# In-projection of a hybrid encoder layer: the first two Strassen products of all sixteen feature pairs ahead of the rest, from un-normalised input

## The chip, the cores and the metric

The kernel runs on one core of a Trainium2 chip. The metric is the time of one launch on the device in microseconds. Of the kernel before there are three timed runs, with a median of 1248.74 us (1247.93 to 1249.16), and one profiled execution.

## The reference

One layer over 1024 tokens of width 1024, all in float32. What matters here is its beginning:

```python
h    = rms_norm(x, norm_mix_pre)          # x * rsqrt(mean(x^2)) * gain
proj = h @ w_in                           # 1024 x 1024 by 1024 x 4096
q, k, v, u, gates = split(proj, [512, 1024, 1536, 2048])
y_a  = chunk_band_attention(q, k, v, rel_bias) @ w_attn_out
y_b  = multiscale_pool(u, w_pool_group, pool_scale) @ w_pool_out
g_a, g_b = split(sigmoid(gates + b_gate), 2)
x = x + rms_norm((g_a * y_a + g_b * y_b) @ w_o, norm_mix_post)
x = x + rms_norm(conv_gated_ffn(rms_norm(x, norm_ffn_pre)), norm_ffn_post)
```

The scale of a row, rsqrt(mean(x^2)), is one number per token. A product with the un-normalised input times the gain can therefore be multiplied by the token's scale afterwards.

## The kernel before

Features lie on partitions and tokens along the free axis. w_in has 32 blocks of 128 features; they are worked on in 16 pairs (`IN_PAIRS`): pairs 0 to 3 and 8 to 11 are blocks of the gates, 4 and 5 of u, 6 and 7 of v, 12 to 15 one block of q with one of k. The input is cut into quadrants B11, B12, B21, B22 (first index: half of the 1024 input features; second: half of the tokens), and the weights of a pair into w11, w12, w21, w22. Float32 precision comes from splitting each operand into a high and a low part (`split`, `split_w`: the cast to the high part on ScalarE, the low part by a subtraction on VectorE). One product of a 128x512 weight block with a 512x512 operand is then 12 matmuls (`mm3`): four blocks of the inner dimension, each high by high, high by low, low by high.

A pair would need eight such products; the class `Pair` makes seven, after Strassen and Winograd: p1 = w11·B11, p2 = w12·B21, p5 = s1·T1, p6 = s2·T2, p3 = s4·B22, p7 = s3·T3, p4 = w22·T4. Here s1 to s4 are sums of the weight blocks (`first`, `sums`, on GpSimd, for the first pairs on VectorE) and T1 to T4 differences of quadrants. Products accumulate in a bank of PSUM where their sum is wanted: p1, p6, p7 and p4 in bank X, p5 and p3 in bank Y, p2 in bank Z. p1 is copied out of X (c1), p1 + p6 as u2, p5 as c5; the four results are evicted as p1 + p2, Y + u2, X + c5 and X. `run_pair` sets the order p1, p2, p6, p3, p7, then p5 of the next pair, then p4.

Pairs 0 and 1 are not made that way. They are done first, by eight products per pair (192 matmuls, line 414, tiles `i`), from un-normalised input for all four quadrants (XR), since the scales of the rows (`scales`, `spread`, tiles R0 and R1 for the two halves of the tokens) are not there yet; the eviction multiplies by R. Then the input is normalised, the operands B11, B21 and T1 to T4 are made, and pairs 2 to 15 run. Pairs 4 and 5 are begun early: their p1 and p2 run in bank m while VectorE makes T1 and T2, their c1 is kept in SBUF, and p6 later starts a new sum, to which VectorE adds c1 at the evictions (line 248 and others).

The gates go through a sigmoid and into DRAM (sig_d, stores from ScalarE's queue), q and k are split and stored, v is transposed, u is stored and read again for the pooled path, whose products (mxp) stand between pairs 8 to 12. The weights of a pair (`win`, 1 MB) are loaded from SP's queue, which works in order, into a ring of six buffers that later also holds the pooled results. The order of each engine comes out of a planner that goes by priorities and expected durations; `high_priority` pulls a block forward. After the in-projection come attention, the output products and the FFN, whose up-projection uses the same class `Pair`, with three pairs begun early.

## Time and profile before

| | us |
|---|---|
| median of three runs | 1248.74 |
| the profiled execution | 1248.39 |
| its span, first to last instruction | 1246.6 |
| TensorE (PE) busy | 1231.2 |
| VectorE (DVE) busy | 939.8 |
| ScalarE (ACT) busy | 657.3 |
| GpSimd (POOL) busy | 282.9 |
| first matmul | 6.71 |
| attention's first scores (pst) | 332.02 |

The granted clock of TensorE is 0.999 over the span. Busy time of TensorE is from the start of a matmul to its end with overlaps counted once, so the share of 99% says that it hardly ever waited, not that it could go no faster. L414 is line 414 of the kernel before; the lines 78, 79 and 86 are in the helpers `split` and `mm3` and belong to every product, so that the tile's name tells which one: `X_i` is bank X of the in-projection, `X_u` that of the up-projection. In names, wh and wl are the high and low parts of weights, xq a quadrant of the input, `first` and `wfirst` the weights of the first products.

### The profile page before, as it was taken

To read this page: it belongs to the slowest core of one execution; us is meant where nothing else is said; L and a number is where in the kernel's file an instruction comes from. 1 tells how busy PE (TensorE), PEld (TensorE's weight loads), DVE (VectorE), ACT (ScalarE), POOL (GpSimd) and SP (SyncE) were. 2 spreads that over 40 slices of the span, in tenths; PEclk is the share of its full clock that TensorE was granted. 3 is DMA by queue.
4 is the path that set the end of the run, shared out by engine and by line. 5 is a ranking of instruction groups with operands and counts; after the bars stand their busy time and mean duration, and the time that the engine had idled before them with its cause. 6 is when DMAs were issued, how large, how long until landed. Compare 5 with 4: busy or idle time off the path is not lost.

```text
span 1246.6 us, 16208 instructions
## 1 busy us (share of the span) xinstructions
PE 1231.2 (99%) x5756; PEld 1023.7 (82%) x5756; DVE 939.8 (75%) x1503; ACT 657.3 (53%) x1149; POOL 282.9 (23%) x229
## 2 busy tenths in 40 slices
PE   7999999999999999999999999999999999999997
PEld 6888888888889888888788888888888888888886
DVE  5996346876588887756799988666676676899968
ACT  6663345564487774434545555455545555445553
POOL 0004222232255546000003443334334300000000
PEclk9999999999999999999999999999999999999999
DMA  9336024335988746412344333122231216903103
GB/s 355 138 131 231 26 89 184 129 131 188 297 277 269 263 154 242 152 73 86 112 148 153 130 110 126 61 102 73 79 101 56 88 68 221 377 18 101 35 1 136
DMA packets 57329, 178.11 MB, mean 143 GB/s; under 512 B 5344, under 2 KB 5984, under 8 KB 52384
## 3 DMA queue, kind: packets, MB, share of 16 engines
q1 hardware_dynamic: 51264, 164.23, 37.3%
q10 hardware_dynamic: 4752, 8.39, 1.8%
q0 software_dynamic: 1232, 4.46, 0.9%
q8 instruction: 45, 0.74, 0.2%
q14 instruction: 36, 0.29, 0.1%
HBM read 128.30 MB, written 48.76 MB: 142 GB/s over the span
## 4 chain that ended last, share of the span: by engine, by line
PE 89%; DVE 8%; issue 1%; ACT 1%; DMA 0%; DVEq 0%; SPq 0%; ACTq 0%
PE X_u L86 16%; PE X_i L86 12%; PE Y_u L86 9%; PE X L86 7%; PE wops L1063 7%; PE Y_i L86 6%; PE i L414 4%; PE Z_u L86 4%; PE y L86 4%; PE ybp L86 4%; PE Y L86 3%; PE Z_i L86 3%; PE f L863 3%; PE tp L838 2%; PE m_u L86 2%; PE pst L795 2%
## 5 line engine op out<-in xcount | busy, mean ns | idle before, releaser
L1187 DVE SCALAR_TENSOR_TENSOR hc<-hu,cv,hc 128x1022 f32<-128x1022 f32 (+1 forms) x88 | 122.7, 1396 | 27.0 <-ACT hc L1182 26.8
L78 ACT CAST wh_u<-s_u 128x512 fp32r<-128x512 f32 x88 | 54.4, 619 | 92.4 <-PE X_u L86 41.7
L79 DVE TENSOR_TENSOR wl_u<-s_u,wh_u 128x512 fp32r<-128x512 f32 x88 | 66.5, 757 | 30.0 <-ACT wh_u L78 30.0
L79 DVE TENSOR_TENSOR wl_i<-s_i,wh_i 128x512 fp32r<-128x512 f32 x56 | 42.7, 763 | 37.3 <-ACT wh_i L78 37.1
L78 ACT CAST wh_i<-s_i 128x512 fp32r<-128x512 f32 x56 | 34.6, 622 | 59.9 <-PE X_i L86 21.9
L78 ACT CAST wh_u<-wup 128x512 fp32r<-128x512 f32 x60 | 37.3, 622 | 52.3 <-PE Y_u L86 27.3
L1182 ACT ACTIVATE hc<-hu,cv 128x1024 f32<-128x1024 f32 x44 | 54.6, 1244 | 12.2 <-DVE hu L1131 11.4
L208 POOL TENSOR_TENSOR s_u<-s_u,wup 128x512 f32<-128x512 f32 x19 | 26.6, 1403 | 131.1 <-DVE wl_u L79 131.1
L204 POOL TENSOR_TENSOR s_u<-wup 128x512 f32<-128x512 f32 x19 | 33.7, 1775 | 74.7 <-DVE wl_u L79 74.7
L204 POOL TENSOR_TENSOR s_i<-win 128x512 f32<-128x512 f32 x11 | 15.9, 1446 | 150.8 <-DVE wl_i L79 112.8
L817 POOL TENSOR_SCALAR pe<-pe,st 128x640 f32<-128x640 f32 (+4 forms) x58 | 40.3, 699 | 42.2 <-DVE st L815 28.3
L813 ACT ACTIVATE pe<-sm,st 128x640 f32<-128x640 f32 (+2 forms) x64 | 44.3, 694 | 8.1 <-DVE st L811 7.8
L79 DVE TENSOR_TENSOR ptl<-tp,pth 128x512 fp32r<-128x512 f32 (+3 forms) x80 | 43.0, 552 | 7.4 <-ACT pth L78 6.6
L210 POOL TENSOR_TENSOR s_u<-wup 128x512 f32<-128x512 f32 x19 | 40.7, 2141 | 27.2 <-DVE wl_u L79 27.2
L1192 ACT ACTIVATE hc<-hc 128x1024 f32<-128x1024 f32 x22 | 23.4, 1062 | 39.8 <-DVE hc L1187 39.8
L78 ACT CAST pth<-tp 128x512 fp32r<-128x512 f32 (+3 forms) x80 | 36.4, 474 | 14.8 <-PE tp L838 10.5
L86 PE MATMUL ybp<-mx,wh_yb 128*128 128x512 f32 x128 | 43.4, 414 | 0.0
L78 ACT CAST wh_i<-win 128x512 fp32r<-128x512 f32 x38 | 23.4, 622 | 37.4 <-PE X_i L86 22.8
L79 DVE TENSOR_TENSOR wl_u<-wup,wh_u 128x512 fp32r<-128x512 f32 x60 | 42.1, 702 | 0.7
L811 DVE CUSTOM_DVE_ANT_0 sm<-pst,bt 128x640 f32<-128x640 f32 (+2 forms) x64 | 40.5, 651 | 2.7 <-issue 1.5
L863 PE MATMUL f<-ptl,vv 128*128 128x256 f32 x144 | 36.5, 287 | 0.0
L838 PE MATMUL tp<-ident,pe 128*128 128x128 f32 x240 | 36.2, 275 | 0.1
(503 smaller groups left out, 4169.9 us busy)
## 6 DMA issues: line engine op xcount, KB each, us to landing
wup<-in_w_up SPq DMA_DIRECT2D x22, 1024.0 KB, 5.0
win<-in_w_in SPq DMA_DIRECT2D x14, 1024.0 KB, 5.8
g_d<-hc SPq DMA_DIRECT2D x20, 512.0 KB, 2.7
sig_d<-d ACTq DMA_DIRECT2D x32, 256.0 KB, 2.0
a<-g_d SPq DMA_DIRECT2D x8, 1024.0 KB, 10.9
b<-in_w_dn SPq DMA_DIRECT2D x8, 1024.0 KB, 12.3
x<-in_xn SPq DMA_DIRECT2D x8, 512.0 KB, 11.5
v_d<-vt SPq DMA_DIRECT2D x8, 512.0 KB, 3.1
```

The costliest lines, as they stand in the source:

```text
L78: r = A.copy(hi, src)
L79: (eng or V).tensor_tensor(lo, src, hi.bitcast(F32), ALU.subtract)
L86: nc.tensor.matmul(ps, a[i], b[i], start=start and i == 0 and p == 0, stop=stop and i == n - 1 and p == 2, skip_group_check=True,)
L204: self.eng.tensor_tensor(self.s1, self.w21, self.w22, ALU.add)
L210: self.eng.tensor_tensor(self.s3, self.w11, self.w21, ALU.subtract)
L414: nc.tensor.matmul(acc[b, t], w[:, b], x[:, k], start=i == k == p == 0, stop=i == 1 and k == 3 and p == 2, skip_group_check=True)
L813: A.activation(pe[:, :n], sm[:, :n], AF.Exp, scale=-1.0, bias=st[:, 0:1], accum_out=st[:, 1:2])
L838: nc.tensor.transpose(tp[:, c * P:(c + 1) * P], pe[:, b * P:(b + 1) * P], ident)
L863: nc.tensor.matmul(fo, vv[:, kb, e].rearrange("p a d -> p (a d)"), t[:, s], start=s == slots[0] and x == 0, stop=s == slots[-1] and x == 1)
L1063: nc.tensor.matmul(ps[:, 512 * c:512 * c + 512], a[k // 4][:, k % 4, sl], wo[k][b][:, 512 * c:512 * c + 512], start=k == 0 and x == 0, sto ...
L1182: A.activation(c, hu, AF.Identity, scale=cv[:, C_CW + 88 + b:C_CW + 89 + b], bias=cv[:, C_CB + b:C_CB + b + 1])
L1187: V.scalar_tensor_tensor(c[:, n:], hu[:, :S - n], cv[:, w:w + 1], c[:, n:], ALU.mult, ALU.add)
```

## The change

The two pairs of plain products are gone; all sixteen pairs are made of seven products. But p1 and p2 of all pairs are run first, in a stage of their own:

- The first 96 matmuls are p1 and p2 of pairs 0 to 3, from the un-normalised input of the first half of the tokens (XR, only B11 and B21). p1 goes to banks X and Y, p2 to Z and m; ScalarE copies p1 out (c1), VectorE adds both.
- For pairs 4 to 15, p1 and one product later p2 accumulate in one bank (X, Y and Z in turn), with p1 copied out between them. The eviction multiplies the sum by R0. Half of a pair's weights (`w12`, 512 KB) is loaded for this.
- c1 of each pair is stored to DRAM (c1_d, ScalarE's queue), un-normalised.
- R0, R1, the normalised quadrants and the operands T1 to T4 and B22 are made during this stage.
- Then each pair runs its other five products, p6, p3, p7, p5 of the next pair, p4. c1 is loaded back (SP's queue, one buffer), and VectorE writes c1·R0 into bank X before p6, which accumulates onto it. So u2 and c5 become plain copies on ScalarE, as for a pair that is not early.
- XR lies where attention's first two heads have their operands later; these are loaded from q_d and k_d (`load_head`) after pair 14 in program order.
- The FFN's three early pairs get c1 into the bank in the same way, by a copy on ScalarE without a scale (`seed`).
- The pooled path stands two pairs apart, at pairs 6, 8, 10 and 12.

In the whole program TensorE has 5732 matmuls in place of 5756.

```diff
@@ class Pair
+        def begin(self, w, c1):
             self.early, self.c1 = True, c1
+            if w is None:
+                return
         def p1(self):
             if self.early:
-                self.X = self.bank("m")
+                self.X = self.bank(self.tags[0])
...
         def p2(self):
+            if self.tags != "mm":
+                self.prod(self.X, self.w12, "B21", False, "2")
+                self.evict(0, 0, self.X, None)
+                return
...
         def p6(self):
             if self.early:
                 self.X = self.bank("X")
-            self.prod(self.X, self.s2, "T2", self.early, "6")
-            if self.early:
+            if self.scale is not None:
+                V.tensor_tensor(self.X, self.c1, self.scale, ALU.mult)
+            elif self.seed:
+                A.copy(self.X, self.c1)
+            self.prod(self.X, self.s2, "T2", self.early and not self.seed, "6")
+            if self.early and not self.seed:
                 V.tensor_tensor(self.u2, self.X, self.c1, ALU.add)
             else:
                 A.copy(self.u2, self.X)
...
@@ the in-projection
-        XR = {(0, 0): two("T1", "XR00")}
+        XR = [(hd.tile([P, 4, 512], F32R, tag=f"qk{i}", name=f"XRh{i}"),
+               Halves(*[hd.tile([P, 2, 512], F32R, tag=f"{x}{i}", name=f"XRl{i}{x}") for x in ("kl", "bt")]))
+              for i in range(2)]
...
+        def load_w12(n):
+            w12[n] = tmp.tile([P, 1024], F32, tag="o", bufs=4, name=f"w12_{n}")
+            nc.sync.dma_start(w12[n], w_in[n][:, :1024])
...
+        def keep_p1(n):
+            A.dma_start(c1_d[n], pairs[n].c1)
+
+        def turn(n):
+            p = pairs[n]
+            p.weights(raws[n])
+            p.c1 = tmp.tile([P, 512], F32, tag="c1", name=f"c1b_{n}", bufs=1)
+            nc.sync.dma_start(p.c1, c1_d[n])
+            p.scale = Rb[0]
+            p.evict = evict_in(IN_PAIRS[n])
+            return p
+
+        acc = [[psp.tile([P, 512], F32, tag=tag, name=f"first{i}{b}") for b, tag in enumerate(t)]
+               for i, t in enumerate(("XXYY", "ZZmm"))]
+            for i in range(2):
+                for k in range(4):
+                    split_raw(i, k)
+                    products(acc[i], i, k)
+            for n in range(4):
+                A.copy(begin(n).c1, acc[0][n])
...
+            scales(0)
+        sums = [wr[0][:, n] for n in range(4)]
+        for n in range(4):
+            V.tensor_tensor(sums[n], acc[1][n], pairs[n].c1, ALU.add)
...
+        for n in range(5, NP):
+            if n + 3 < NP:
+                load_w12(n + 3)
...
+            p.p1()
+            keep_p1(n)
+            with tc.high_priority():
+                p.prep("2", p.w12)
+            pairs[n - 1].p2()
+            for x in extra.get(n, ()):
+                x()
...
+        for pi in range(2, NP):
+            for n in (pi + 1, pi + 2):
+                if n < NP and n not in raws and (pi < 9 or n == pi + 1):
+                    load_win(n)
+            if pi in (7, 11):
+                    mx[x].append(rawp.tile([P, 2, S], F32R, tag="raw", name=f"mx{x}{pi}"))
+            after = turn(pi + 1) if pi + 1 < NP else None
+            run_pair(pair, after,
+                     {"p6": lambda: split_yb(0), "p7": lambda: split_yb(1)} if after is None else (), True)
...
+            if pi == 14:
+                load_head(0)
+                load_head(1)
@@ the FFN's early pairs
-            p.evict, p.first_product, p.early_prep = evict, first, prep
+            p.evict, p.first_product, p.early_prep, p.seed = evict, first, prep, True
```

The queue of SP around the last pairs' weights. Before (win13 to win15 are the weights of pairs 13 to 15, wg the pooled path's weights, u its input, q_d and k_d stores of results):

```order
L521 DMA u3_2043<-u_d_69 128x1024
L545 DMA wg2_2189<-in_w_pg 128x128
L337 DMA win13_2230<-in_w_in 128x2048
L472 DMA q_d_66<-hl_2270 128x2x512
L545 DMA wg3_2386<-in_w_pg 128x128
L337 DMA win14_2408<-in_w_in 128x2048
```

The same stretch with the change (c1b_13 and c1b_14 are the c1 of pairs 13 and 14 on their way back, qk0 the first head's q):

```order
L553 DMA u3_2453<-u_d_69 128x1024
L577 DMA wg2_2429<-in_w_pg 128x128
L622 DMA c1b_13_2455<-c1_d_74 128x512
L622 DMA c1b_14_2592<-c1_d_74 128x512
L378 DMA win13_2451<-in_w_in 128x2048
L503 DMA q_d_66<-hl_2497 128x2x512
L378 DMA win14_2590<-in_w_in 128x2048
L503 DMA k_d_67<-hl_2520 128x2x512
L359 DMA qk0_2846<-q_d_66 128x1024
```

The loads of c1 for two pairs now stand ahead of the weights of pair 13, and the first load for a head among the stores.

VectorE at the same place with the change (X_i13 is the bank of pair 13 into which c1·R0 is written; wl_5_i13 the low part of the weights s1 of its p5; d31_1 and d0_1, d4_1 evictions of pairs 11 and 12):

```order
L530 TENSOR_TENSOR d31_1_2381<-X_i11_2326,p5_i11_2264 128x512
L80 TENSOR_TENSOR wl_3_i12_2480<-s4_i12_2386,wh_3_i12_2479 128x512
L80 TENSOR_TENSOR wl_7_i12_2502<-s3_i12_2387,wh_7_i12_2501 128x512
L256 TENSOR_TENSOR X_i13_2597<-c1b_13_2455,R0_361 128x512
L80 TENSOR_TENSOR mx111_2320<-mo2_2439,mx011_2319 128x512
L530 TENSOR_TENSOR d0_1_2495<-Y_i12_2391,u2_i12_2459 128x512
L502 SCALAR_TENSOR_TENSOR hl_2497<-d0_1_2495,hl_2497 128x512
L80 TENSOR_TENSOR wl_5_i13_2533<-s1_i13_2457,wh_5_i13_2532 128x512
L530 TENSOR_TENSOR d4_1_2517<-X_i12_2460,p5_i12_2392 128x512
```

The write into the bank stands among the splits and evictions of the pair before; in the order of the kernel before there is no such row, and in its place stand the splits of p1 and p2 of each pair (wl_1, wl_2).

385 lines of the change are left out of this document (167 added, 218 removed).

## The prediction

> **What bounds the kernel now.** I read first the page's busy times, then the list of waits for TensorE (engine, line, releaser: total us, times, longest), then the chain of waits over the in-projection.
>
> ```profile
> PE 1231.2 (99%) x5756; PEld 1023.7 (82%) x5756; DVE 939.8 (75%) x1503; ACT 657.3 (53%) x1149; POOL 282.9 (23%) x229
> PE i L414 <- ACT w0s L78: 6.7, 1, 6.7
> PE X_u L86 <- ACT wh_u L78: 0.5, 1, 0.5
> PE X_i L86 <- ACT u_i L250: 0.4, 1, 0.4
> ```
>
> TensorE is busy for 1231.2 of 1246.6 us, and of the 15.4 us it is not, 6.7 us are the start. No later wait is longer than 0.5 us. Every matmul taken away therefore shortens the run by its pace, as long as no new wait takes its place. The pace stands in the chain (start, duration, what) and in TensorE's timeline:
>
> ```profile
> 6.71 22.21 PE i L414 x84
> 109.15 2.72 PE Y_i L86 x12
> 31.96 0.63 PE L414 MATMUL i<-XR01h,w0s 128*128 128x512 f32 x2
> 44.19 0.60 PE L433 MATMUL rps<-ident,bc 128*128 128x128 f32 x4
> 44.55 0.71 PE L414 MATMUL i<-XR01h,w0s 128*128 128x512 f32 x2
> 54.56 0.39 PE L86 MATMUL X_i<-B11h,wh_i 128*128 128x512 f32 x1
> ```
>
> A product of 12 matmuls takes 2.72 us, so one matmul 0.2267 us. The 0.39 us of the single matmul in the last row is its latency, not its pace; I do not use it. The second half of the plain products (96 matmuls, token half 1) runs from 31.96 to 54.56: 22.60 us, of which 0.36 (44.19 to 44.55) are the four small transposes, against 96 x 0.2267 = 21.76. So this loop loses 0.48 us.
>
> Then I asked how near the other engines are to being late, by windows (window, length, then busy us with counts of PE, PEld, DVE, ACT, POOL, then clock, share of DMA, GB/s):
>
> ```profile
> 30.00:100.00 70.00, 70.00 (x311) 57.70 (x310) 67.77 (x96) 47.72 (x71) 0.01 (x1) 1.00 0.44 161
> 90.00:170.00 80.00, 80.00 (x355) 66.30 (x354) 40.62 (x58) 28.19 (x46) 22.89 (x17) 1.00 0.31 112
> 250.00:332.00 82.00, 81.96 (x361) 67.45 (x360) 53.09 (x71) 42.67 (x73) 21.80 (x16) 1.00 0.56 188
> 332.00:350.00 18.00, 18.00 (x112) 15.80 (x111) 16.20 (x49) 12.45 (x32) 6.96 (x16) 1.00 0.89 291
> 680.00:700.00 20.00, 19.11 (x84) 15.20 (x83) 19.89 (x22) 9.91 (x14) 7.38 (x4) 1.00 0.51 171
> ```
>
> From 30 to 100 us VectorE is busy 67.77 of 70 us and TensorE still never waits. From 90 us on VectorE is half idle, and the DMA engines are half idle until attention starts at 332.
>
> **The change, part by part.**
>
> *Fewer matmuls.* Before: two pairs by plain products (192 matmuls) and 14 pairs of seven products (14 x 84 = 1176), together 1368. After: 16 pairs of seven products, 16 x 84 = 1344; the first 96 of these are p1 and p2 of pairs 0 to 3. That is 24 fewer: -24 x 0.2267 = **-5.44 us**.
>
> *The slow loop.* The 22.60 us loop is gone and its work done in products at the pace of 2.72 us: **-0.48 us**. The other half, 6.71 to 31.96, stays as it is in order and operands (weights and input arrive in the same order, except one 512 KB load ahead of the row-wise input, which only the row scales need).
>
> *The row scales.* R0 and R1 are now computed while p1 and p2 of pairs 4 to 7 run. Their transposes on TensorE take 0.36 us each before and after. The new thing is what R0 stands behind: on ScalarE its root comes after the copy of p1 of pair 4.
>
> ```profile
> L219 ACT COPY p_i<-Y_i 128x512 f32<-128x512 f32 x12 | 7.0, 580 | 0.4 <-ACT d L503 0.4
> 22.30 0.30 ACT L302 ACTIVATE rs_s<-ssq,eps 128x4 f32<-128x4 f32 x1
> 23.64 0.43 DVE L430 COPY bc<-rst 128x512 f32<-128x512 f32 x1
> ```
>
> The first 96 matmuls end near 31.6 (31.96 less the transposes, which move), p1 of pair 4 near 34.4. Copy 0.58, root 0.30, from the root's end (22.60) to the copy bc (23.64) 1.04, and 0.43 for it: 36.8 us. TensorE comes to the transposes, which stand behind 10 matmuls of p1 of pair 5, at 31.6 + 2.72 + 2.27 = 36.6. Bounds for such a wait: 0, if matmul and copy overlap, and 1 us, if the squares of the rows are late by that; 0.3 for R0, by the sum and a little for the signals between the engines, and the same for R1, which is placed likewise: **+0.6 us**.
>
> *VectorE in the stage of first products.* It adds p1 and p2 of pairs 0 to 3, multiplies 16 first blocks by R0, splits 24 weight blocks, normalises the input and makes the T operands. From row 20 of its order up to the split of the weights that p6 of pair 1 needs, I count 101 instructions: 7 subtractions and 8 splits of 128x1024 (T1, T2, B22, T3) at 1.22 us, 16 normalisations at 0.745, 56 others of 128x512 at 0.68 to 0.76 (38.8 us in all), 12 tiny steps of the row scales and two copies bc (about 2.4 us together):
>
> ```profile
> L79 DVE TENSOR_TENSOR wl_i<-s_i,wh_i 128x512 fp32r<-128x512 f32 x56 | 42.7, 763 | 37.3 <-ACT wh_i L78 37.1
> L440 DVE SCALAR_TENSOR_TENSOR xq<-xq,gn,R 128x512 f32<-128x512 f32 x16 | 11.4, 745 | 3.0 <-ACT R L435 3.0
> L462 DVE TENSOR_TENSOR xq<-xq,xq 128x1024 f32<-128x1024 f32 x8 | 9.5, 1221 | 0.0
> ```
>
> The sum is 71.4 us. It has from 31.5 to about 109.8 us, 78.3 us. Before, 67.8 of 70 us were carried without a wait; so 71.4 of 78.3 should be: 0. If VectorE does come late, the cover is gone and each us goes to TensorE (rival B).
>
> *p1 into the bank.* Before each p6 VectorE writes c1 x R0 into the bank. No row shows this form; it is a 128x512 write with two inputs, as below, so 0.69 us (between the copy's 0.58 on ScalarE and 1.22 for twice the size). It replaces nothing on TensorE, and in the stretch from 90 us VectorE is half idle:
>
> ```profile
> L248 DVE TENSOR_TENSOR u_i<-X_i,c 128x512 f32<-128x512 f32 x2 | 1.4, 692 | 2.5 <-PE X_i L86 2.5
> ```
>
> There are two X banks. The bank of p6 of pair n is free when p4 of pair n-2 has been evicted, a full pair (five products, 13.6 us) earlier. Cost 0 as long as the c1 load is there: 256 KB land in about 2.0 us (the row sig_d below), one issued per pair.
>
> *The queue of SP, the one place where I expect a new wait.* The loads of c1 stand in SP's order between the 1 MB weight loads, and there is one buffer for them. The load c1b_14 must wait for VectorE's write X_i13 from c1b_13; that must wait until ScalarE has read p4 of pair 11 from the bank. Behind c1b_14 stands win13, whose own buffer is free some 11 us before. Before, no pair's weights stood behind such a load:
>
> ```profile
> 246.62 0.33 SPq L337 DMA_DIRECT2D win<-in_w_in  x1
> 269.93 0.57 SPq L337 DMA_DIRECT2D win<-in_w_in  x1
> 287.16 0.34 SPq L337 DMA_DIRECT2D win<-in_w_in  x1
> 276.10 1.82 POOL L204 TENSOR_TENSOR s_i<-win 128x512 f32<-128x512 f32 x1 [10.39 <-DMA win<-in_w_in]
> 292.36 1.50 POOL L204 TENSOR_TENSOR s_i<-win 128x512 f32<-128x512 f32 x1 [7.91 <-DMA win<-in_w_in]
> L503 ACT ACTIVATE d<-d,cv 128x512 f32<-128x512 f32 x18 | 13.0, 724 | 10.6 <-DVE d L485 10.2 <-DVE s_i L208 0.4
> L78 ACT CAST wh_i<-win 128x512 fp32r<-128x512 f32 x38 | 23.4, 622 | 37.4 <-PE X_i L86 22.8 <-PE Y_i L86 10.1 <-PE i L414 4.2
> win<-in_w_in SPq DMA_DIRECT2D x14, 1024.0 KB, 5.8
> sig_d<-d ACTq DMA_DIRECT2D x32, 256.0 KB, 2.0
> ```
>
> The last two win loads of before took 276.10 - 269.93 = 6.2 and 292.36 - 287.16 = 5.2 us until GpSimd began, and GpSimd already waited for them; p1 and p2 of the same pair (5.44 us) covered that. Now they come first and no longer cover it. Call t the end of p4 of pair 11. Sigmoid 0.72, seed 0.69, two issues 0.33 each: win13 starts near t + 2.0 or 2.1. With 5.2 to 6.2 us to land, 1.5 for s1 on GpSimd, 0.62 for the cast and 0.69 for the low part, of which the first two matmuls cover 0.45, p5 of pair 13 may start at t + 4.4 + landing, t + 9.6 to t + 10.6. It is due at t + 1.36 (six pooled matmuls) + 3 x 2.72 = t + 9.5. So a wait of 0.1 to 1.1 us; I take 0.7, by the median landing of 5.8: **+0.7 us**. Queued behind it on ScalarE are the casts of p4 of pair 12, and on VectorE its evictions; all of them move with TensorE. Bounds: 0 if the load is quick, 6.9 if it takes the 12 us that a load takes under a full DMA (rival A). The weights of pairs 14 and 15 are issued some 5 us before they would be late, so I cost them at 0.
>
> *More traffic.* c1 out and back (16 x 256 KB each way, 8.4 MB), half-weights of ten more pairs (5.2 MB), full weights of pairs 0 and 1 (2.1 MB): 15.7 MB in 325 us, 48 GB/s on top of 110 to 190, at a DMA share of 0.3 to 0.56. Hidden, with the exception above. ScalarE issues 16 stores more (about 0.4 us each, 6.4 us): it is busy 47.7 of 70 us, so that too is hidden.
>
> *Attention's heads.* They are loaded earlier. TensorE was busy 18.00 of 18 us from 332 on, so nothing is gained.
>
> *FFN.* Three early pairs there get c1 copied into the bank by ScalarE and lose VectorE additions. From 680 to 700 VectorE is full (19.89 of 20) and TensorE 0.89 short. Bounds 0 to -0.9; since only nine additions go, I take **-0.3 us**.
>
> Sum: -5.44 - 0.48 + 0.6 + 0.7 - 0.3 = **-4.92 us**. The profiled execution took 1248.39 (span 1246.6 and 1.8 around it); it would take 1243.5, the span 1241.7. The median of the runs, 1248.74, is 0.35 above the profiled one: 1248.74 - 4.92 = **1243.8 us**.
>
> **The rivals.** About 0.2%, 2.5 us, is what a measurement of this kernel can tell from no change.
>
> *A, slower: a late load of win13 stalls TensorE.* Place: p5 of pair 13. The stage from 250 us on has a DMA share of 0.56; at five products per pair in place of seven the same weights and stores come in 5/7 of the time, with c1 loads on top and the heads' loads next to it: share near 0.8. For: with a share of 0.89 after 332 us a 512 KB load took 12.0 us.
>
> ```profile
> sgb<-sig_d SPq DMA_DIRECT2D x2, 512.0 KB, 12.0
> 6.71 2.07 PE L414 MATMUL i<-XR00h,w0s 128*128 128x512 f32 x4 [6.71 <-ACT w0s L78]
> 13.09 1.09 PE L414 MATMUL i<-XR00l,w0s 128*128 128x512 f32 x4
> ```
>
> At 12 us the wait is 4.4 + 12 - 9.5 = 6.9 in place of 0.7: 1243.8 + 6.2 = 1250.0. After a long wait TensorE may start slow, as at the beginning: the 16 matmuls that started from 6.71 to 13.09 took 6.38 us in place of 16 x 0.2267 = 3.63, 2.75 more. I count that in, since nothing shows that it stays away: 1252.8, which is slower. It decides (8.1 us of wait, slow start included) from a landing of 10.5 us. Against: the load's own row has a median of 5.8. The Trainium skill, "TensorE: Matmul & The Clock Gate", section "HAM oscillation — how this bites in real kernels", says that a TensorE idle for more than about 3.4 us falls back to half clock and has to warm up again; by that the wait of 6.9 us gives the 1252.8, and one of 0.7 us costs nothing beside itself. No row after the start shows a gap that long, so the trace agrees only in that the slow matmuls stand right behind the first one.
>
> *B, no change that can be measured: VectorE is late.* Place: between 90 and 115 us, where the split of T3 and T4, the sums of weights for pairs 0 to 2 and the first two seeds meet. On average VectorE stood idle for 37.3 / 56 = 0.67 us before a split of weights, waiting for ScalarE's cast. If 16 of this stage's splits wait like that, 10.7 us, the reserve of 78.3 - 71.4 = 6.9 us is used up and 3.8 go to TensorE: 1247.6. For: VectorE is the fullest engine there, and works in order. Against: instructions that stand back to back come in less than their 0.69 us,
>
> ```profile
> 95.01 0.69 DVE L79 TENSOR_TENSOR wl_i<-s_i,wh_i 128x512 fp32r<-128x512 f32 x1
> 95.61 0.69 DVE L485 TENSOR_TENSOR d<-X_i,p_i 128x512 f32<-128x512 f32 x1
> ```
>
> 0.60 from start to start, and those 0.67 us are from the stage in which VectorE is half idle.
>
> *C, the full gain.* No new wait: -5.44 - 0.48 - 0.9 = -6.8, so 1241.9. For: margins I called close are all positive. Against: win13.
>
> *D, the change doesn't do what it says.* TensorE's order holds 5732 matmuls in place of 5756, so the 24 are gone; that leaves no time for this rival.
>
> **How the numbers follow.** Forecast (waits of 0.5 to 3 us): 0.58, 1242.5 to 1245.9. C: 0.13. B: 0.19, of which 0.05 still end faster than 1246.2. A: 0.10, of which 0.08 end above 1251.2. Faster by over 0.2% (below 1246.2): 0.58 + 0.13 + 0.05 = 0.76; within: 0.14 + 0.02 = 0.16; slower: 0.08. The range: C's end less a little, 1241, up to 1249.5, which takes in B with its uncertainty; it leaves out A and the far end of C.
>
> **What would show it.** The matmul rows of the in-projection sum to 1344 and attention's first scores (pst) start near 327 in place of 332.0. TensorE's list of waits has one entry for Y of p5 with the low or high part of s as releaser, 0 to 1.2 us, and GpSimd's s1 waits for DMA win at pair 13 longer than before. VectorE is near 95% busy from 30 to 100 with no wait of TensorE behind it. The window 680 to 700, moved by the shift, has less than 0.9 us idle. Wrong would be: a wait of TensorE for VectorE between 90 and 115 us of more than 2 us (B), or one of more than 3 us near pair 13 (A), or a pace of products other than 2.72 us.

## The result, and the profile after

The changed kernel takes 1261.06 us (median; 1258.28 to 1264.13), the kernel before beside it 1248.40 (1247.23 to 1249.16). The ratio is 1.0102, with a 95% interval of 1.0087 to 1.0116: slower by 1.0%, 12.7 us, where 4.92 us less were predicted. The profiled execution took 1261.29, its span is 1259.5. One of the four runs of experiment 1 below took 2071.72 us at a mean granted clock of 0.557, and its median is that of the other three.

Busy times of the page after, to be held against 1231.2 us of PE and a span of 1246.6 before:

```profile
PE 1228.8 (98%) x5732; PEld 1018.8 (81%) x5732; DVE 934.6 (74%) x1500; ACT 662.0 (53%) x1167; POOL 300.3 (24%) x236
```

The 24 matmuls are gone and PE is busy for 2.4 us less, but it is now idle for 30.7 us in place of 15.4. The list of waits for TensorE after (releaser: total us, times, longest) says for whom:

```profile
PE first L454 <- ACT w0s L79: 6.9, 1, 6.9
PE Y_i L87 <- ACT wh_i L79: 4.6, 1, 4.6
PE X_i L87 <- DVE d L530: 3.8, 2, 2.7
PE X_i L87 <- ACT u_i L263: 3.3, 2, 2.2
PE X_u L87 <- DVE hu L1150: 1.3, 2, 0.8
PE vps L544 <- DVE vt L80: 1.1, 1, 1.1
PE Y_i L87 <- DVE wl_i L80: 0.8, 1, 0.8
PE mxp L87 <- DVE pdl L80: 0.6, 1, 0.6
PE rps L473 <- DVE bc L470: 0.5, 2, 0.3
```

Before, no wait but the first was over 0.5 us. Now there is one of 4.6 and a row of them from 0.6 to 2.7, for VectorE or for ScalarE. Those of the in-projection lie in two places (hu belongs to the FFN). The windows after (columns as in the prediction):

```profile
100.00:205.00 105.00, 105.00 (x471) 86.80 (x470) 50.73 (x79) 44.25 (x76) 35.02 (x25) 1.00 0.48 168
205.00:320.00 115.00, 105.38 (x463) 84.85 (x462) 85.86 (x112) 58.03 (x99) 46.04 (x27) 1.00 0.50 172
320.00:343.00 23.00, 18.42 (x71) 14.59 (x70) 8.33 (x13) 7.95 (x14) 2.18 (x3) 0.85 0.79 266
```

and the same from the trace before:

```profile
100.00:205.00 105.00, 105.00 (x481) 86.97 (x480) 48.36 (x72) 38.92 (x68) 31.94 (x24) 1.00 0.29 110
205.00:320.00 115.00, 114.54 (x501) 93.59 (x500) 82.69 (x113) 63.94 (x110) 32.65 (x22) 1.00 0.46 161
```

Up to 205 us TensorE is full in both. From 205 to 320, while the pooled path runs, it loses 9.6 us, and here VectorE is busy for 85.9 of 115 us and GpSimd for 46.0 in place of 32.7. In the last 23 us before attention it loses another 4.6, and the clock granted is 0.85.

The ledger goes by TensorE's rows, from start to start, each matmul at its pace of 0.2267 us; "lost" is what lies over that:

| | us |
|---|---|
| fewer matmuls and the slow loop, as predicted | -5.44 - 0.48 |
| first matmul at 6.91 in place of 6.71 | +0.2 |
| two waits for the row scales (35.2, 49.9) | +0.32 + 0.47 |
| two short losses of before (225.8, 267.5) that are gone | -0.77 |
| six losses beside the pooled path, 213.8 to 315.7 | 1.27 + 2.36 + 1.29 + 2.87 + 0.73 + 1.21 = +9.7 |
| p5 of pair 13 at 285.2, the wait foreseen | +1.0 |
| p3 of pair 15 at 327.9: wait, then slow matmuls | 4.74 + 2.5 = +7.2 |
| sum | +12.3 |

Measured: the first p6 of the up-projection starts 11.7 us later (650.8 for 639.1). 0.6 of the sum is not accounted for. From there to the last p6 (1033.4 for 1020.7) it loses 1.0 more, so the FFN's early pairs cost time and don't gain 0.3.

**The place at 327.9.** TensorE's timeline after, with the wait in brackets:

```profile
327.92 0.39 PE L87 MATMUL X_i<-T2h,wl_i 128*128 128x512 f32 x1
332.89 0.80 PE L87 MATMUL Y_i<-B22h,wh_i 128*128 128x512 f32 x1 [4.58 <-ACT wh_i L79]
...
338.14 0.39 PE L87 MATMUL X_i<-T3h,wh_i 128*128 128x512 f32 x1
```

Twelve matmuls take from 332.89 to 338.14, 5.25 in place of 2.72 us. ScalarE's cast of the weights, which TensorE names, came late because in ScalarE's order an unrelated cast stood ahead of it and waited for a load:

```profile
331.70 0.62 ACT L79 CAST wh_yb<-wr_yb 128x512 fp32r<-128x512 f32 x1 [4.78 <-DMA wr_yb<-in_w_po]
```

wr_yb is the first weights of an output product. They had been asked for at 303.72 before, and are now asked for 20 us later. SP's queue after, in its order:

```profile
310.95 6.82 SPq L503 DMA_DIRECT2D k_d<-hl  x2
317.82 0.59 SPq L362 DMA_DIRECT2D qk<-k_d  x1
...
321.22 0.36 SPq L503 DMA_DIRECT2D q_d<-hl  x1
...
323.20 0.36 SPq L503 DMA_DIRECT2D k_d<-hl  x1
323.65 0.52 SPq L593 DMA_DIRECT2D wr_yb<-in_w_po  x1
```

and the one row of before:

```profile
303.72 0.35 SPq L565 DMA_DIRECT2D wr_yb<-in_w_po  x1
```

The heads' loads (qk, and kl between the rows shown), moved from attention's code into the in-projection, and the stores of k and q, which wait for VectorE to finish hl, now stand ahead of it.

**The place at 234.6**, one of the six beside the pooled path. VectorE after, then ScalarE, GpSimd and TensorE in their own order:

```profile
228.74 0.15 DVE L562 COPY pl<-u 128x1 f32<-128x1 f32 x1 [3.32 <-DMA u<-u_d]
228.81 1.96 DVE L563 TENSOR_TENSOR pl<-u 128x1023 f32<-128x1023 f32 x1
230.69 0.68 DVE L80 TENSOR_TENSOR wl_i<-s_i,wh_i 128x512 fp32r<-128x512 f32 x1
231.37 1.21 DVE L563 TENSOR_TENSOR pl<-pl 128x1022 f32<-128x1022 f32 x1
232.50 1.77 DVE L80 TENSOR_TENSOR wl_i<-s_i,wh_i 128x512 fp32r<-128x512 f32 x1
235.40 0.15 DVE L568 TENSOR_TENSOR pl<-pl,u 128x3 f32<-128x3 f32 x1
...
235.58 1.04 ACT L79 CAST pdh<-pl 128x1024 fp32r<-128x1024 f32 x1 [4.98 <-DVE pl L568]
236.53 0.58 ACT L263 COPY u_i<-X_i 128x512 f32<-128x512 f32 x1
...
231.45 2.27 POOL L211 TENSOR_TENSOR s_i<-win 128x512 f32<-128x512 f32 x1 [1.76 <-DVE wl_i L80]
...
237.16 0.50 PE L87 MATMUL X_i<-T3h,wh_i 128*128 128x512 f32 x1 [2.20 <-ACT u_i L263]
```

VectorE stands 3.3 us at the load of u, then works through the pooled sums. ScalarE, in order too, stands 5.0 us at the cast of their result, and behind it stands the copy of u2 that frees TensorE's bank X. The same split takes 0.68 us at 230.69 and 1.77 at 232.50, while GpSimd adds weights from 231.45 to 233.72.

### The profile page after: what moved, and what is told of

Its sections match the earlier page's. It is cut to its first block, busy times and chain, and to the rows that moved or that the text cites. A ratio compares the mean times of both kernels' runs of the same rounds, so it can differ in the third digit from the quotient of the medians.

```text
span 1259.5 us, 16285 instructions
## 1 busy us (share of the span) xinstructions
PE 1228.8 (98%) x5732; PEld 1018.8 (81%) x5732; DVE 934.6 (74%) x1500; ACT 662.0 (53%) x1167; POOL 300.3 (24%) x236
## 4 chain that ended last, share of the span: by engine, by line
PE 78%; DVE 12%; DMA 3%; issue 3%; ACT 2%; POOL 1%; SPq 0%; DVEq 0%; ACTq 0%; POOLq 0%
PE X_u L87 15%; PE X_i L87 8%; PE Y_u L87 8%; PE X L87 7%; PE wops L1082 7%; PE Y_i L87 6%; PE Z_u L87 4%; PE y L87 4%; PE Y L87 3%; PE ybp L87 3%; PE f L883 3%; PE tp L858 2%; PE m_u L87 2%; PE Z_i L87 2%; PE pst L815 1%
## 5 line engine op out<-in xcount | busy, mean ns | idle before, releaser
L79 ACT CAST wh_i<-s_i 128x512 fp32r<-128x512 f32 x64 | 39.6, 621 | 70.7 <-PE X_i L87 20.5
L80 DVE TENSOR_TENSOR wl_i<-s_i,wh_i 128x512 fp32r<-128x512 f32 x64 | 51.3, 808 | 33.5 <-ACT wh_i L79 33.4
L205 POOL TENSOR_TENSOR s_i<-win 128x512 f32<-128x512 f32 x13 | 23.7, 1821 | 174.2 <-DVE wl_i L80 122.8
L883 PE MATMUL f<-pth,vv 128*128 128x256 f32 x144 | 36.5, 285 | 0.0
```

Source lines behind the costliest of these rows:

```text
L79: r = A.copy(hi, src)
L80: (eng or V).tensor_tensor(lo, src, hi.bitcast(F32), ALU.subtract)
L205: self.eng.tensor_tensor(self.s1, self.w21, self.w22, ALU.add)
L883: nc.tensor.matmul(fo, vv[:, kb, e].rearrange("p a d -> p (a d)"), t[:, s], start=s == slots[0] and x == 0, stop=s == slots[-1] and x == 1)
```

## The experiments

Two theories for the two places. For the place at 327.9: wr_yb is asked for late because of what was put ahead of it in SP's queue; rivals are its traffic or ScalarE. For the stage from 205 to 320: the pooled path, on a VectorE that has less room per pair (five products, 13.6 us, in place of seven, 19.0), holds up what TensorE waits for, whether by its amount, by its place in the orders of VectorE and ScalarE, or because GpSimd's additions stretch VectorE's instructions. Unless said otherwise the numbers are medians, and ratios are to the kernel before.

**1. wr_yb asked for at the start of pair 14**, into buffers that are free by then.

```diff
+        def load_first_yb():
+            for m in range(2):
+                w = out_tile(f"wr_yb{m}").rearrange("p (k n) -> p k n", k=4)
+                nc.sync.dma_start(w, w_po[m])
+                wr_ybs.append(w)
...
+            if pi == 14:
+                load_first_yb()
```

> The changed kernel, with the two weight blocks of the pooled output (wr_yb) in two other buffers of SBUF and requested at the start of pair 14, ahead of the loads of the second head in SP's queue. Theory 1 (the wait of 4.74 us near 328, and the slow matmuls after it, come from ScalarE standing at the cast of a wr_yb that SP's queue requested late): the wait of Y_i for wh_i is gone or under 1 us, attention starts 5 to 7 us earlier than the 343.6 us of the changed kernel, time 1254 to 1257. Rival (the last pairs are late anyway, since VectorE and ScalarE are behind): another wait of about the same size takes its place, time above 1259.

1254.32, ratio 1.0048 (1.0031 to 1.0064): 6.7 less than the change. The wait of 4.6 and the slow matmuls behind it are gone; the other waits stay, some of them shorter. So this place costs about what the ledger says, 7.2 us. The agreement is only rough: the profiled execution of 1 has slow matmuls in two places of the pooled stage, from 237.4 and from 305.7 us on, about 3 us in all, where that of the change has none (the last section says when they come).

**2. The heads' loads back in attention's code**, nothing else.

```diff
-            if pi == 14:
-                load_head(0)
-                load_head(1)
...
+            load_head(0)
             load_yb(0)
...
+        load_head(1)
```

> The changed kernel with the loads of attention's first two heads requested where they were before the change, after the in-projection in program order; nothing else differs. Theory 1a (it is these loads, moved in front, that hold wr_yb back in SP's queue): the wait of 4.7 us near 328 is gone or under 1 us, as with the early wr_yb, time 1254 to 1257. Rival 1b (it is the stores of q and k, which wait in the same queue for VectorE's low parts): the wait stays above 3 us, time 1258 to 1262.

1256.48, ratio 1.0069 (1.0042 to 1.0096). SP's queue of this kernel:

```profile
314.94 1.56 SPq L503 DMA_DIRECT2D k_d<-hl  x2
316.59 0.45 SPq L593 DMA_DIRECT2D wr_yb<-in_w_po  x1
```

wr_yb is asked for 7 us sooner and its wait is gone, with 4.6 us. It is still behind the two stores of k (before: 303.72), but ahead of the second head's loads of k (325.80) and of the last stores of q and k (322.68 and 325.38). So moving the loads is what made it too late; how much of the 7 us is the loads' own and how much that of the stores between them is not separated. A wait of 2.2 us for the pooled product came in place of one of 0.6, which is most of what 2 gains less than 1 (2.2 us).

**3. The pooled sums left out**; the path's loads, splits and products stay.

```diff
             src = u
-            step = 1
-            while step < w:
...
-            V.scalar_tensor_tensor(src[:, e:], src[:, e:], 1.0 / w, u[:, e:], ALU.mult, ALU.subtract)
             hi = tmp.tile([P, S], F32R, tag="o", bufs=4, name=f"pdh{m}")
```

> The changed kernel without the trailing sums, the mean and the subtraction of the pooled path: its input u is split into high and low part directly, so the pooled branch is not computed. All its loads, casts and products stay. Theory 2 (the waits between 210 and 316 us, about 9 us, come from the pooled path's long VectorE chain, behind which ScalarE stands at the cast pdh and VectorE's own evictions stand in line): the waits at pairs 8, 9, 10, 12 fall from 8.5 to under 3 us, time 1253 to 1256, the wait for wr_yb stays. Rival (the order of SP's queue, late win and u loads): these waits stay within 2 us of what they are, time 1259 to 1262.

1252.28, ratio 1.0031 (1.0018 to 1.0044): 8.8 less. Its waits:

```profile
PE Y_i L87 <- ACT wh_i L79: 5.6, 2, 5.0
PE X_i L87 <- DVE d L530: 1.0, 1, 1.0
PE Y_i L87 <- DVE wl_i L80: 0.8, 1, 0.8
```

Of the pooled stage one wait of 1.0 is left, beside that of pair 13; the place at 327.9 is as before.

**4. c1 loaded from GpSimd's queue**, so that win13 has no c1 load ahead of it.

```diff
-            nc.sync.dma_start(p.c1, c1_d[n])
+            G.dma_start(p.c1, c1_d[n])
```

> The changed kernel with the loads of c1 on GpSimd's queue in place of SP's, so that no weights stand behind them; the order of TensorE is the same. Theory 3 (c1b_14 ahead of win13 in SP's queue costs the wait of 0.84 us at p5 of pair 13, and no more): that wait is gone, time 0.5 to 1.5 us lower, 1259.5 to 1260.5. Rival (the lateness of win13 also sets the waits after it, at pairs 13 and 14): 3 us or more lower, under 1258. If GpSimd's sums come later because its queue waits at these loads: slower than 1261.

1259.71, ratio 1.0094 (1.0078 to 1.0109). The times alone (1259.52 to 1261.07, against 1258.28 to 1264.13) don't separate that from the change. The trace does: GpSimd's s1 of pair 13 starts at 277.46 in place of 282.88, and the wait at pair 13 (0.8) is gone. The prediction's step on win13 was right in place, and near in size by the ledger (1.0 for 0.7).

**5. No seed in the FFN's early pairs**, as in the kernel before.

```diff
-            p.evict, p.first_product, p.early_prep, p.seed = evict, first, prep, True
+            p.evict, p.first_product, p.early_prep = evict, first, prep
```

> The changed kernel with the three early pairs of the FFN as before (no copy of c1 into the bank, c1 added at the evictions by VectorE). Theory 4 (the copies cost ScalarE and the order there more than VectorE gains; the waits between 640 and 760 us are 1.9 us in place of 1.2): the waits are 1.2 again, time 0.5 to 1 us lower, 1260 to 1260.5. The prediction's term (-0.3): 0.3 us higher.

1260.03, ratio 1.0094 (1.0079 to 1.0110). The times alone don't separate that from 1261.06. The trace does: the up-projection's X products run from 650.0 to 1031.7, 381.7 us, as before (381.6), where the change took 382.6.

**6. Edits 1, 4 and 5 together.**

```diff
+            if pi == 14:
+                load_first_yb()
...
+            G.dma_start(p.c1, c1_d[n])
...
+            p.evict, p.first_product, p.early_prep = evict, first, prep
```

> The changed kernel with wr_yb early, the loads of c1 on GpSimd's queue, and the FFN's early pairs as before, all together. If the three causes are separate, their gains add: 1261.1 - 6.2 - 1.4 - 1.0 = 1252.5, and the waits that are left are those of the pooled path (8 us or so). If they are one cause seen in three places, less: above 1254.

1251.97, ratio 1.0028 (1.0017 to 1.0039). The three differences, 6.7, 1.35 and 1.0, make 9.1 us, and 9.1 are measured; that it fits so closely is luck, as the last two lie within the spread of the runs. What is left is the pooled stage; the following kernels start from this one.

**7. The same without the pooled sums** (edit 3).

```diff
-            while step < w:
...
             src = u
```

> The kernel with all three repairs and without the trailing sums, the mean and the subtraction of the pooled path (the pooled branch is not computed; loads, casts and products stay). If the four causes are the whole of the loss and the prediction's terms for matmuls and the slow loop are right, the time is 1252.5 - 8.8 = 1243 to 1245, below the kernel before by about 4 us. If the shorter pair (13.6 us) has too little room for VectorE and ScalarE in general: other waits come up, above 1247.

1243.18, ratio 0.9958 (0.9942 to 0.9973). With the pooled sums out of the way this is near what the prediction gave: 1243.8, or 1243.4 without its terms for win13 (+0.7) and the FFN (-0.3), since the edits 4 and 5 take out what these stand for.

**8. The split of the pooled result on VectorE alone**, so that ScalarE never stands at it.

```diff
-            split(hi, lo, src)
+            V.tensor_copy(hi, src)
+            V.tensor_tensor(lo, src, hi.bitcast(F32), ALU.subtract)
```

> The kernel with all three repairs, and both parts of the pooled result split on VectorE (a copy in place of ScalarE's cast pdh). Theory 2a (ScalarE, standing at pdh until VectorE's chain is done, holds back its copies and casts for TensorE): the wait for u_i goes, 2 to 4 us lower than with the three repairs alone, 1249 to 1250.5. Theory 2b (VectorE itself is late, its evictions stand behind the chain): the same or up to 2 us slower, since VectorE gets about 1.1 us more for each of the four.

1252.95, ratio 1.0035 (1.0021 to 1.0049), no better than 6. TensorE's waits for VectorE's evictions rise to 7.4 us in four. So ScalarE standing at pdh is a link of the chain and not all of it. How much of the lateness is VectorE's own this run does not separate, since VectorE got the copy as additional work.

**9 and 10. The pooled path started earlier**, at pairs 5, 6, 8, 10 (9) and 5, 7, 9, 11 (10), with the buffers it shares with the weights taken earlier too. The edit of 10:

```diff
-            if pi in (7, 11):
+            if pi in (6, 10):
...
-            m = {6: 0, 8: 1, 10: 2, 12: 3}.get(pi)
+            m = {5: 0, 7: 1, 9: 2, 11: 3}.get(pi)
```

> The kernel with the three repairs, and the pooled path at pairs 5, 6, 8 and 10 in place of 6, 8, 10 and 12 (its results get their buffers earlier, so from pair 8 on weights are requested one pair ahead only). If the pooled waits come from where the path meets other VectorE work (q and k splits from pair 12 on, vt at 8): 3 to 5 us lower than with the three repairs, 1247 to 1249. If they come from the length of its chain wherever it stands: within 1.5 us of 1252, with the same waits at other pairs. If the weights are late, GpSimd's s1 waiting for win: slower than 1252.

> The same with the pooled path at pairs 5, 7, 9 and 11: each two pairs apart as in the change, but one pair earlier, the longest sums (window 16) ahead of the q and k pairs. By place: the wait of 2.7 us at pair 13 goes, 1248.5 to 1250. By length of chain: within 1.5 us of 1252.

1254.54, ratio 1.0048 (1.0033 to 1.0063), and 1252.34, 1.0031 (1.0020 to 1.0043): no gain. The waits are gathered in one place: in 10 one of 5.9 us has come, and the others of the stage sum to 1.8 us. TensorE there, then ScalarE and VectorE in the time before:

```profile
275.21 0.79 PE L87 MATMUL Y_i<-T1h,wh_i 128*128 128x512 f32 x1 [5.94 <-ACT wh_i L79]
275.81 0.63 PE L87 MATMUL Y_i<-T1l,wh_i 128*128 128x512 f32 x1
...
272.37 0.72 ACT L523 ACTIVATE d<-d,cv 128x512 f32<-128x512 f32 x1 [7.92 <-DVE d L530]
...
264.64 3.47 DVE L80 TENSOR_TENSOR mx<-mo,mx 128x512 fp32r<-128x512 f32 x2
```

The cast that TensorE names stands in ScalarE's order behind the sigmoid of an eviction, for which ScalarE waits 7.9 us, and VectorE comes to that eviction (271.65) only behind the pooled sums and two splits mx, which take 3.47 us beside GpSimd's additions (0.69 us each in experiment 13, without them). 9 has the same at 263.1 us. So this is the pooled path again, at another place. The weights do come late too, since the pooled results lie in their ring: GpSimd waits 12.2 us for win at 281.45, but no wait of TensorE over 1.1 us follows. Here a long wait is again followed by slow matmuls.

**11. The pairs' work at high priority**, ahead of the pooled path wherever the planner has a choice.

```diff
-            run_pair(pair, after,
...
+            with tc.high_priority():
+                run_pair(pair, after,
```

> The kernel with the three repairs, the five products of each pair, with their splits and evictions, planned at a higher priority than the pooled path, which stays at pairs 6, 8, 10 and 12. In VectorE's order this changes little (the evictions of pair 13 still stand behind two or three of the path's additions), so by length of chain 1250.5 to 1252.5; if it is only the order of equal instructions that matters, under 1249.

1285.27, ratio 1.0291 (1.0276 to 1.0307). A miss that tells little: TensorE's own order changed with it, p7 now stands right behind p4, and it waits ten times, 14.7 us in all, for ScalarE's copy u_i.

**12. The pooled path cut into single steps**, one after each of p6, p7 and the end of pairs 6 to 13, the widest window first.

```diff
-        def pooled_path(m, u):
+        def pooled_steps(m):
...
+            while step < w:
+                add(step)
                 step *= 2
+                yield None
+            fin()
+            yield None
+            part()
+            yield None
+            pooled_out(m, *st["pd"])
...
+            go = (lambda: next(pooled, None)) if 6 <= pi < 14 else (lambda: None)
             run_pair(pair, after,
-                     {"p6": lambda: split_yb(0), "p7": lambda: split_yb(1)} if after is None else (), True)
+                     {"p6": lambda: split_yb(0), "p7": lambda: split_yb(1)} if after is None else
+                     {"p6": go, "p7": go}, True)
```

> The kernel with the three repairs, and the pooled path cut into single steps (one addition, the mean, the split, the product), of which one stands after p6, after p7 and at the end of each pair from 6 to 13; the longest sums (window 16) come first, the shortest last, and the pooled results get their buffers at pairs 8 and 11. If the pooled waits come from several of its operations standing together ahead of an eviction in VectorE's order, they fall from 7.5 to under 3 us: 1245 to 1248, not slower than the kernel before. If VectorE, ScalarE and GpSimd together have no room for the path in pairs of 13.6 us, however it is cut: 1250 to 1253, the waits at other places.

1249.66, ratio 1.0012 (1.0003 to 1.0021): 2.3 less than 6. Of what is left 2.3 us are one wait for the small weights of the pooled product (wgl), with slow matmuls behind it.

**13. GpSimd's sums of weights left out**, for pairs 3 to 15: the products run on the weight blocks themselves, so that TensorE, VectorE and ScalarE have the same work. It also spares the time that a sum takes to arrive.

```diff
         def first(self):
+            if self.eng is G and self.name[0] == "i":
+                self.s1 = self.w21
+                return
...
         def sums(self):
+            if self.eng is G and self.name[0] == "i":
+                self.s2, self.s4, self.s3 = self.w11, self.w12, self.w22
+                return
```

> The kernel with the three repairs and without GpSimd's sums of weights: from pair 3 on, the blocks w21, w11, w12, w22 themselves are taken in place of s1 to s4 (the in-projection's second half is wrong by that). The pooled path stays whole at pairs 6, 8, 10, 12. If the stretching of VectorE's operations by GpSimd's additions is what makes the pooled path late, the waits fall from 7.5 to under 3 us, 1244 to 1247.5, and VectorE's 128x512 splits there take 0.7 us throughout. If it is the path's own operations, standing together in VectorE's order: the waits stay above 5 us, 1249.5 to 1252.

1242.73, ratio 0.9955 (0.9940 to 0.9970). With the pooled path untouched, every wait of the stage is gone. The groups of VectorE from 205 to 318 us, first of the change, then of this kernel:

```profile
L80 DVE TENSOR_TENSOR wl_i<-s_i,wh_i 128x512 fp32r<-128x512 f32 x28 | 26.8, 964 | 8.4 <-ACT wh_i L79 8.2
L256 DVE TENSOR_TENSOR X_i<-c1b,R 128x512 f32<-128x512 f32 x7 | 7.0, 1004 | 2.7 <-ACT d L523 2.3 <-ACT d L532 0.4
L530 DVE TENSOR_TENSOR d<-X_i,p_i 128x512 f32<-128x512 f32 x7 | 4.8, 683 | 2.8 <-PE X_i L87 2.8
```

```profile
L80 DVE TENSOR_TENSOR wl_i<-win,wh_i 128x512 fp32r<-128x512 f32 x38 | 25.8, 686 | 15.7 <-ACT wh_i L79 15.7
L262 DVE TENSOR_TENSOR X_i<-c1b,R 128x512 f32<-128x512 f32 x7 | 4.9, 696 | 3.8 <-ACT d L529 2.3 <-ACT d L538 1.5
L536 DVE TENSOR_TENSOR d<-X_i,p_i 128x512 f32<-128x512 f32 x8 | 5.5, 688 | 3.1 <-PE X_i L87 3.1
```

A split of weights falls from 964 to 686 ns, the write of c1·R0 into the bank from 1004 to 696; the eviction, which reads one input from PSUM, takes 683 and 688. So a running GpSimd addition lengthens these instructions, which read both inputs from SBUF, and not the eviction. A copy within SBUF, with one input, is lengthened as well: the pooled path's copies of 128x2 take 886 ns on average in the change and 163 in this kernel. The 28 splits and 7 writes of the change lose 28 x 0.278 + 7 x 0.308 = 9.9 us of VectorE's time by it.

**14 and 15. The two halves of a remedy.** 14 is 12 with the small weights loaded and split with the pooled result, and a fourth step per pair from pair 9 on:

```diff
             def part():
+                wg = tmp.tile([P, P], F32, tag="S", bufs=4, name=f"wg{m}")
+                nc.sync.dma_start(wg, w_pg[m])
...
+            go4 = go if pi > 8 else (lambda: None)
-                     {"p6": go, "p7": go}, True)
+                     {"p1": go4, "p6": go, "p7": go}, True)
```

> The pooled path in single steps as in the run spread, with the small weights of its products requested and split together with its result instead of just before the product, and one step more per pair from pair 9 on, so that nothing of it is left for the pairs of q and k but one product. If the wait of 2.3 us at pair 13 came from the late small weights alone, it goes: 1246.5 to 1248.5, level with the kernel before or just below. If a denser path brings the waits back: 1249 to 1252.

1248.11, ratio 0.9997 (0.9988 to 1.0006). 15 is 6 with the sums of pairs 7 to 12 moved from GpSimd to VectorE:

```diff
-            p = Pair(None, T, psp, tmp, f"i{n}", None, 6, V if n < 3 else G)
+            p = Pair(None, T, psp, tmp, f"i{n}", None, 6, V if n < 3 or 7 <= n < 13 else G)
```

> The kernel with the three repairs, with the weight sums s1 to s4 of pairs 7 to 12 on VectorE in place of GpSimd (nothing left out; TensorE's order is the same). VectorE gets 24 operations of 0.6 to 0.69 us (15 us in some 82 us), and its other operations should no longer be stretched (0.69 in place of 0.91 us for a split). If stretching by GpSimd makes the path late: 1245 to 1248.5. If the total of work on VectorE does: 1252 or slower.

1249.84, ratio 1.0011 (1.0002 to 1.0020). Each takes 2 to 4 us away from 1251.97, neither is enough. 15 takes the stretching away only in part: its longest wait, 2.72 us at 302.15, stands behind the last pooled sums, beside which GpSimd still adds the weights of pair 14, and the splits there take 1.78 us.

**16 and 17. Misses on the way**: 14 without the fourth step, alone and with the sums of pairs 7 to 12 on VectorE.

```diff
-            go4 = go if pi > 8 else (lambda: None)
+            go4 = lambda: None
```

> The pooled path in single steps, three per pair as in the run spread, with its small weights requested and split together with its result. If the 2.5 us lost at pair 13 came from the small weights alone: 1246 to 1247.5, below the kernel before by 1 to 2 us. If not: 1248 to 1250.

> spread3 with the weight sums of pairs 7 to 12 on VectorE. By the stretching, the waits fall further: 1243.5 to 1246.5, below the kernel before by more than 2 us. By the total of work: 1249 or slower.

1251.16, ratio 1.0020 (1.0012 to 1.0029): the pooled product of pair 13 waits 2.3 us for its low part. 1248.32, ratio 0.9994 (0.9985 to 1.0003).

**18. Both halves: 14 with the sums of pairs 7 to 13 on VectorE.**

```diff
-            p = Pair(None, T, psp, tmp, f"i{n}", None, 6, V if n < 3 else G)
+            p = Pair(None, T, psp, tmp, f"i{n}", None, 6, V if n < 3 or 7 <= n < 14 else G)
```

> The run spread2 with the weight sums of pairs 7 to 13 on VectorE. By the two causes (path crowded in VectorE's order, VectorE stretched by GpSimd) both shrink: 1244.5 to 1247, below the kernel before by 1.5 to 4 us. If only the total of work on VectorE counts: 1248 to 1250.

1243.30 (1243.01 to 1243.98), ratio 0.9958 (0.9945 to 0.9972): 0.4% faster than the kernel before and 1.4% faster than the change, with all the work done. Its longest waits in the in-projection behind the first, its window and its splits:

```profile
PE rps L473 <- DVE bc L470: 1.5, 2, 1.4
PE X_i L87 <- DVE d L530: 0.6, 1, 0.6
```

```profile
205.00:320.00 115.00, 113.63 (x504) 93.06 (x503) 89.06 (x137) 63.86 (x108) 16.94 (x15) 1.00 0.60 202
```

```profile
L80 DVE TENSOR_TENSOR wl_i<-s_i,wh_i 128x512 fp32r<-128x512 f32 x31 | 22.4, 729 | 10.7 <-ACT wh_i L79 10.6
```

VectorE is busier in that window than in the change (89.1 for 85.9 of 115) and TensorE waits for 1.4 us in it in place of 9.6. 14 differs from 18 only in where these sums of weights run: VectorE is as busy in 14 (88.9), and 14 is 4.8 us slower. So it was not the amount of VectorE's work. It was that its work came in lumps, with instructions stretched by GpSimd just then. Either one taken away whole is enough (7 and 13, though 13 also spares the arrival of the sums); a part of one alone was not (12, 14, 15). Whether moving pair 13's sums too was needed in 18 is open: 14 with those of pairs 7 to 12 alone was not run.

## Why the prediction was wrong

Right were: the 24 matmuls and the slow loop (-5.92); the row scales, +0.79 for +0.6; win13, 1.0 lost for 0.7, and that it is c1's load ahead of it (4); that TensorE doesn't wait for VectorE from 51 to 205 us, so rival B's place was not one. Without the other new waits the change takes about what was forecast: 1243.18 in 7, 1243.30 in 18, for 1243.8, or 1243.4 without the two terms that both kernels lack.

Three steps failed.

"From 90 us on VectorE is half idle", with the write of c1·R0, the pooled path and the splits there at cost 0. The windows quoted were 90 to 170 and 250 to 332, and the second already has VectorE busy for 53.1 of 82 us, 65%, which is not half idle. The stretch between was not quoted; over 205 to 320 the trace before had VectorE busy for 82.7 of 115 us, 72%. A mean was also the wrong view: a pair shrinks from 19.0 to 13.6 us while the pooled path keeps its size, and its steps stand in one lump in two in-order queues. And the write was priced at 0.69 us, and took 1.00 beside GpSimd; the quoted rows had the sign of it, splits that read s at 763 ns. In place of 0 the trace showed 9.7 us lost, and 8.8 us go when the pooled sums are left out (3).

"They are loaded earlier ... so nothing is gained", of the heads' loads. The gain was rightly nothing; what they are moved past was not asked. In SP's order they stand ahead of wr_yb, and ScalarE casts wr_yb ahead of TensorE's weights. 7.2 us in the ledger, 6.7 by experiment 1. This is rival A's mechanism, a load late behind SP's queue and slow matmuls after the wait (2.75 named, 2.5 measured), at another load. A's price, 6.2 + 2.75 = 9.0, was near; its place, win13, was wrong: A and its chance of 0.10 were weighed for one load, and the queue held more of them.

The FFN's -0.3 was +1.0: ScalarE's copy of c1 into the bank is not free there, and VectorE's hu, which TensorE waits for (1.3 us in two), comes later with it than without. Which of ScalarE's instructions is late was not followed further.

The change therefore does what it says; most of what it lost came from work whose amount it left as it was, the pooled path and the cast of wr_yb, and that lost its cover as the pairs became shorter or its place in a queue.

## What to carry to other kernels

When a stage is made shorter, go through what keeps its size in it (here the pooled path and the stores), and ask stretch by stretch, for each in-order engine, what now stands ahead of the instruction that frees TensorE; a mean over 80 us hides it. A load that moves up in a queue costs what it is moved past: find the next transfer behind it and who casts it. On VectorE, price an instruction with both inputs in SBUF at its length beside GpSimd, and where VectorE is the engine waited for, an addition of weights may be cheaper on VectorE itself than on GpSimd.

## What the runs showed of the hardware

How much GpSimd lengthens VectorE's instructions was not expected: 964 for 686 ns on average, single splits 1.77 for 0.68 us, while those that read PSUM stay at 0.68 to 0.69. GpSimd's additions take longer beside VectorE's work too, from 1.29 us up to 5.22:

```profile
228.40 1.29 POOL L210 TENSOR_TENSOR s_i<-win,s_i 128x512 f32<-128x512 f32 x1
306.86 5.22 POOL L205 TENSOR_TENSOR s_i<-win 128x512 f32<-128x512 f32 x1 [5.72 <-DVE wgl L80]
```

The Trainium skill, "SBUF — State Buffer", section "🔬 SBUF: two separate sides", gives the rule: a VectorE instruction with two SBUF inputs and a GpSimd one that reads SBUF take turns on a shared pair of ports, and the later one blocks for the whole of the other. The traces agree for the rows with two SBUF inputs and for the eviction, which has one; 0.68 and one full addition of 1.29 would be 1.97 (an estimate from these rows), and the longest splits took 1.8.

TensorE is slow again after some waits. After those of 4.58 and 5.94 us the next matmuls came 0.43 us apart, 12 and 7 of them, for 0.2267. The Trainium skill, "TensorE: Matmul & The Clock Gate", section "HAM oscillation — how this bites in real kernels", puts the limit at an idle time of about 3.4 us. These runs differ: seven matmuls came at 0.43 us behind a wait of 1.92 us in experiment 1 (236.66) and behind one of 2.72 us in 15 (302.15), and none behind the same 2.72 us in the change (305.34). The granted clock is 0.50 there for 3.41 us, or for two such stretches on end. Windows of that length show the difference, first in experiment 1, then in the change (columns as before, the clock third from the end):

```profile
234.00:237.41 3.41, 1.49 (x7) 0.94 (x6) 2.91 (x5) 2.34 (x5) 0.00 (x0) 1.00 0.27 47
237.41:240.82 3.41, 3.41 (x9) 2.65 (x9) 3.41 (x6) 1.15 (x2) 1.86 (x2) 0.50 0.63 250
```

```profile
300.53:303.95 3.42, 2.10 (x10) 1.40 (x8) 3.42 (x6) 0.00 (x0) 0.61 (x1) 1.00 0.77 205
303.95:307.36 3.41, 2.02 (x9) 1.67 (x10) 3.41 (x8) 0.75 (x1) 0.50 (x1) 1.00 1.01 416
```

The windows are counted in steps of 3.413 us from where the clock of the same trace falls to half (237.41 in experiment 1, 331.25 in the change). The wait of 1.92 us lies in one window whole; that of 2.72 us is parted between two, 1.3 and 1.4 us. Counted so over all traces of this case, from 15 us on and up to the last products, every window at full clock in which TensorE stood idle for 1.92 us or more was followed by half clock, and none with less than 1.7 us; between these some were and some not (1.74 was, 1.89 was not). So a wait of 4.6 us cost 7.2, and whether one of 2 to 3 us costs some 1.5 us more depends on where it falls. Differences of that size between two of the experiments can come from this alone.
